# Weight and activation tiles moved by 64 bytes, and the squares of the norm in another ring: a two-layer decoder trunk on one core

## The chip, the cores and the metric

The kernel runs on 1 core of one Trainium2 chip. The metric is device time in microseconds, from the runs' median. Five engines work side by side, each in the order of its own queue: TensorE (PE, its weight loads shown apart as PEld), VectorE (DVE), ScalarE (ACT), GpSimd (POOL) and SyncE (SP), which issues most transfers.

## What is computed

A trunk of two layers on 512 tokens of width 1024, all in float32. Cut to what matters here:

```python
def hybrid_layer(x, norm_mix, w_in, ..., w_out, norm_mlp, w_up, w_down):
    h = rmsnorm(x, norm_mix)
    proj = h @ w_in                 # 1024 x 4896: queries, keys, values, gates
    ...                             # forgetting attention -> y_a, sparse attention -> y_b
    mixed = jax.nn.sigmoid(gate_a) * y_a + jax.nn.sigmoid(gate_b) * y_b
    x = x + mixed @ w_out
    h = rmsnorm(x, norm_mlp)
    return x + jnp.square(jax.nn.relu(h @ w_up)) @ w_down    # 1024 -> 4096 -> 1024

def reference(x, ...):
    for l in range(2):
        x = hybrid_layer(x, ...)
    return rmsnorm(x, norm_final)

def rmsnorm(x, g):
    return x * lax.rsqrt(jnp.mean(x * x, axis=-1, keepdims=True) + 1e-6) * g
```

## The kernel before

**Layout of the work.** Activations stand transposed: features on the 128 partitions, the 512 tokens along the free axis, so that x is eight tiles of 128 x 512. Every matrix product is made of three products of reduced-precision parts: a value v is split into a high part h (a cast) and a low part v - h, and weight-high by activation-high, weight-high by activation-low and weight-low by activation-high are added in PSUM. In `gemm` these are lines 244, 245 and 246. The activation is the moving operand (128 x 512), the weight block the stationary one (128 x 128).

**Tiles.** `Body.t(tag, shape)` gives out tiles by tag. Each tag has a number of buffers in `BUFS`; tags in `LOCAL` get the part of the program appended, so that "t2" is one ring in the attention of layer 0 ("a0") and another in its output projection and MLP ("m0"). Where a tile lies in SBUF is worked out by the framework's packer at build time: a tag's count limits how many of its tiles are alive, and any tile may be put into bytes whose owner is no longer alive, whatever its tag; it then has to wait for the last use of those bytes. All sizes are multiples of 2048 bytes a partition save one: the tile "tiny" (small vectors and constants) is 6976 bytes, which is 54.5 times 128. In the program before the packer puts the large rings below it, at multiples of 128 bytes (the double tiles "u2", the rings "kd", "kk", "long" and "vn", a part of the "o2" tiles), and the others above it, where every address is 64 past a multiple of 128 (the weight tiles "wh" and "wl", most of "o2", the late activations "a4", the raw weights "e", "f" and "raw").

**The tags that the change touches.**
- "u2" (4 buffers, 8192 bytes): holds u, the normed input's high and low parts, two feature tiles to a buffer, made by `make_u` through `twin` (lines 266 to 279). u is the moving operand of the projections of a layer (`block`, lines 244 to 246) and the stationary one in `token_proj` (lines 368 to 370). In the MLP the same ring holds split weights: in `Strassen.convert` (line 1497) the pairs a11 and a12, s1 and a22, s2 and s4 for the up-projection, in `Strassen.operands` (line 1252, through `twin`) the operands d for the last quarter of the down-projection. The operand s3 goes into a single tile of the ring "zz".
- "a4" (4 buffers, 6144 bytes): the late activations (the last four of the sixteen units), made in `Strassen.act` and moved in `Strassen.down` as a11, a12 and s4; s1, s2, s3 and a22 move the combined tiles "tt".
- "tmp" (3 buffers): short-lived 128 x 512 tiles, among them the squares and their running sum in `sumsq`.
- "t2" (12 buffers a part): the scratch of `Strassen.prepare` in the MLP parts.

**Order of the work around the change.** After the attention, a loop over m from 0 to 7 does the output projection, one feature tile at a time: 24 matmuls, the residual sum on VectorE (line 1094), then `S.prepare(m)`, which makes the Strassen operands of x (line 1424 scales, lines 1416 and 1417 split into high and low), then `sumsq`, which squares x[m] on ScalarE (line 288) and adds the square to the running sum (line 298), on GpSimd unless its argument `last` is set. From m = 4 on a step of the first unit's weight conversion is put between. The MLP's up-projection is done as sixteen Strassen units (`unit`): seven products (`narrow`, line 1523) of 12 matmuls of 128 x 256, with the down-projections of earlier units put between them (`DOWNS`). The last quarter of the down-projection is Strassen's form too (`down`, line 1315). Its end in layer 0 (`whole`) squares and sums x once more, makes u for layer 1 and sends x to memory.

The order of an engine's instructions is the framework's: it starts from the order of the source and lets its planner move ready work ahead.

Of the kernel before, what the change touches and what calls it, by code (L numbers as in the profile page):

```python
# [19 lines left out]
T = 512  # L20
# [117 lines left out]
def run(*gens):  # L138
    for g in gens:
        for _ in g:  # L140
            pass


class Body:
# [13 lines left out]
    def t(self, tag, shape, dt=F32, name=None):  # L158
        if tag in self.TINY:
            n, bufs = self.TINY[tag]  # L160
            o = self.offset[tag] + self.turns[tag] % bufs * n
            self.turns[tag] += 1
            v = self.tiny[:, o:o + int(np.prod(shape[1:]))]
            return v.rearrange("p (a b c) -> p a b c", a=shape[1], b=shape[2]) if len(shape) == 4 else \
                v.rearrange("p (a b) -> p a b", a=shape[1]) if len(shape) == 3 else v
        n = int(np.prod(shape[1:]))
        if tag in ("tmp", "small") and n < T:
            v = self.sb.tile([128, T], dt, name=name or tag, tag=tag, bufs=self.BUFS[tag])[:, :n]
            if len(shape) > 2:
                v = v.rearrange("p (a b) -> p a b", a=shape[1])  # L170
            if len(shape) > 3:
                raise ValueError(shape)
            return v
        bufs = self.BUFS[tag]
        if tag in self.LOCAL:
            bufs = self.BUFS.get(tag + self.part[0], bufs)
            tag += self.part
        return self.sb.tile(shape, dt, name=name or tag, tag=tag, bufs=bufs)


    LOCAL = "f", "kd", "kk", "q2", "vn", "hl", "zz", "pt", "t2", "zc", "tt"
# [99 lines left out]
    def sumsq(self, x, acc, last=False, behind=None):  # L281

        nc = self.nc
        n = x.shape[-1]
        s = self.t("zz" if last == "apart" else "tmp", [128, T], name="sq")[:, :n]
        if behind is not None:
            nc.scalar.copy(s[:, :1], behind[:, :1].bitcast(F32))
        nc.scalar.activation(s, x, AF.Square)
        if not acc:
            self.sums = 0  # L290
            return [s]
        self.sums += 1
        if self.sums == 6 and len(acc) == 1:
            self.table(AF.Sqrt, s)
        if last == "apart":
            return acc + [s]
        o = self.t("tmp", [128, T], name="acc")[:, :n]
        (nc.vector if last else nc.gpsimd).tensor_tensor(o, s, acc[0], op=OP.add)
        return [o] + acc[1:]
# [321 lines left out]
    def compress(self, kc, vc, small, l):  # L621
# [3 lines left out]
        for x, pos in ((kc, "pos_k"), (vc, "pos_v")):  # L625
            t = [self.t("t2", [128, 8, 2, 32], name="ca") for _ in range(2)]
            v = x.rearrange("p (n j r) -> p r j n", j=8, r=2)
            for half in range(2):
                nc.vector.memset(t[half][:, :, 1, 31], 0.0)
                o = OFF[pos] + 8 * half  # L630
                nc.vector.tensor_copy(t[half][:, :, 0, 31], small[:, o:o + 8])
                for h in range(2):
                    for r in range(2):
                        copy = nc.scalar.copy if h else nc.vector.tensor_copy
                        copy(t[half][r * 64:(r + 1) * 64, :, h, :31], v[h * 64:(h + 1) * 64, r, :, half:half + 31])
            A.append(t)
            yield
# [224 lines left out]
    def layer(self, l, u):  # L862
        nc, a = self.nc, self.a
        self.part = f"a{l}"
        wb = a["wb"][l].rearrange("m p k c -> m p (k c)")

        va = [self.p(t) for t in ("S", "S", "PT", "PT")]
        src = [[a["wva"][l, c].rearrange("p j m -> p (j m)")] for c in range(4)]
        if l == 0:
# [6 lines left out]
        run(g)  # L876
        small = self.small
        g2 = [self.p(t) for t in ("mm", "mm", "O", "O")]
        g = self.token_proj([[a["wg2"][l, c].rearrange("p j m -> p (j m)")] for c in range(4)], 288, g2, u)
        VF = []  # L880
        for b in range(NB):
            v = self.t("va", [128, 8, 128], F32R, name="vf")
# [7 lines left out]
        z = self.t("z", [128, NB, 8])  # L890
# [188 lines left out]
        x = [self.t("pt", [128, 2, T], name="x") for _ in range(KT // 2)]  # L1079
        x = [t[:, i] for t in x for i in range(2)]  # L1080
# [8 lines left out]
        acc = []  # L1089
        for m in range(8):  # L1090
            ps = self.bank()
            w = self.weights(a["wout"][l, m].rearrange("p k c -> p (k c)"))
            run(self.gemm(ps, w, 0, mixed))
            nc.vector.tensor_add(x[m], x[m], ps)
            S.prepare(m)
            acc = self.sumsq(x[m], acc, m == 7)
            if m > 3:
                next(conv, None)
        run(conv)
# [539 lines left out]
```

## Time and profile before

| | us |
|---|---|
| median of 3 runs (1528.76 to 1532.7) | 1531.52 |
| the profiled execution, whole | 1529.82 |
| its span, first to last instruction | 1528.0 |
| TensorE busy | 1505.8 |
| VectorE busy | 1153.5 |
| ScalarE busy | 807.9 |
| GpSimd busy | 139.7 |

The span is taken on the device between the first and the last instruction of the program; the 1.8 us more of the execution lie around it. In rows of groups the columns are: source line, engine, operation, output tile <- input tiles (buffer numbers left out), shape of output <- input, count | busy time in us, mean duration in ns | idle time of the engine just before, and what ended it. In rows of the timeline: start in us from the span's start, length in us, engine, line, operation, tiles, shape, count, and in brackets the idle time before with its releaser. Matmuls are pipelined: the duration of one is longer than the step from its start to the next one's start. In rows of waits: who waited for whom: total in us, times, longest.

### The profile page before, as it was taken

The numbers are of one execution on the slowest core, as the hardware profiler recorded it, in microseconds if no ns is written. First come the engines' busy times: TensorE is split into PE (matmuls) and PEld (weight loads), VectorE is DVE, ScalarE is ACT, GpSimd is POOL, SyncE is SP. The second block draws the span as 40 slices with busy tenths as digits, with TensorE's granted clock in tenths as the row PEclk, the third lists the DMA queues.
The fourth block names the chain that finished last, engine by engine and source line by source line (L and its number), as shares of the span: only waits on it lengthen the run. The fifth ranks groups of instructions, "written<-read, shape, count | busy, mean of one in ns | idle before, by whom it ended". The sixth has DMA issues, their size and how long they took to land.

```text
span 1528.0 us, 23442 instructions
## 1 busy us (share of the span) xinstructions
PE 1505.8 (99%) x8766; PEld 1308.7 (86%) x8766; DVE 1153.5 (75%) x2237; ACT 807.9 (53%) x1536; POOL 139.7 (9%) x169
## 2 busy tenths in 40 slices
PE   9999999999989999999999999999999999999998
PEld 8877888888888989999988788888887899999998
DVE  5678979777876776678747789787779677677796
ACT  6465655554664444455444556565547554444455
POOL 1010000000310000010220000000014100000111
PEclk9999999999999999999999999999999999999999
DMA  7664422224655554564167553222346554544532
GB/s 269 163 165 125 138 69 71 68 73 153 189 145 144 146 138 132 143 167 118 55 207 190 151 123 106 83 70 69 104 156 167 131 158 132 147 145 133 137 98 69
DMA packets 73922, 200.51 MB, mean 131 GB/s; under 512 B 9264, under 2 KB 10672, under 8 KB 73808
## 3 DMA queue, kind: packets, MB, share of 16 engines
q1 hardware_dynamic: 58256, 171.19, 35.9%
q0 software_dynamic: 11520, 20.98, 8.0%
q10 hardware_dynamic: 4032, 6.84, 1.3%
q8 instruction: 69, 1.13, 0.3%
q14 instruction: 45, 0.37, 0.1%
HBM read 150.67 MB, written 4.19 MB: 101 GB/s over the span
## 4 chain that ended last, share of the span: by engine, by line
PE 93%; DVE 3%; issue 1%; ACT 1%; DMA 1%; POOL 1%; POOLq 0%; SPq 0%; DVEq 0%; ACTq 0%
PE ps_mm L244 11%; PE ps_mm L245 11%; PE ps_mm L246 11%; PE ps_S L1523 9%; PE ps_PT L1523 6%; PE ps_mm L1523 4%; PE ps_O L244 4%; PE ps_O L245 4%; PE ps_O L246 4%; PE ps_O L612 2%; PE ps_PT L586 2%; PE ps_S L561 2%; PE ps_O L1523 2%; PE ps_S L1315 2%; PE ps_mm L1315 2%
## 5 line engine op out<-in xcount | busy, mean ns | idle before, releaser
L218 ACT CAST wh<-raw 128x1024 fp32r<-128x1024 f32 (+2 forms) x161 | 164.5, 1024 | 145.4 <-PE ps_mm L245 44.6
L219 DVE TENSOR_TENSOR wl<-raw,wh 128x1024 fp32r<-128x1024 f32 (+2 forms) x161 | 191.7, 1191 | 26.0 <-ACT wh L218 25.3
L1504 DVE TENSOR_TENSOR s<-raw,s 128x1024 fp32r<-128x1024 f32 (+1 forms) x128 | 138.7, 1087 | 89.4 <-ACT s L1503 89.1
L244 PE MATMUL ps_mm<-u,wh 128*128 128x512 f32 x480 | 193.9, 404 | 0.0
L246 PE MATMUL ps_mm<-u,wl 128*128 128x512 f32 x480 | 190.8, 397 | 0.0
L245 PE MATMUL ps_mm<-u,wh 128*128 128x512 f32 x480 | 190.8, 397 | 0.0
L1503 ACT CAST s<-raw 128x1024 fp32r<-128x1024 f32 (+1 forms) x128 | 119.1, 940 | 28.4 <-PE ps_mm L1523 17.0
L244 PE MATMUL ps_mm<-o,wh 128*128 128x512 f32 x288 | 113.5, 394 | 0.0
L245 PE MATMUL ps_mm<-o,wh 128*128 128x512 f32 x288 | 113.2, 393 | 0.0
L246 PE MATMUL ps_mm<-o,wl 128*128 128x512 f32 x288 | 113.1, 393 | 0.0
L244 PE MATMUL ps_O<-o,wh 128*128 128x512 f32 x280 | 110.3, 394 | 0.1
L245 PE MATMUL ps_O<-o,wh 128*128 128x512 f32 x280 | 110.2, 393 | 0.0
L246 PE MATMUL ps_O<-o,wl 128*128 128x512 f32 x280 | 110.0, 393 | 0.0
L1523 PEld LDWEIGHTS ps_S<-t,s 128*128 128x128 f32 x768 | 101.2, 193 | 8.4 <-ACT z L1553 3.7
L246 PEld LDWEIGHTS ps_mm<-u,wl 128*128 128x128 f32 x480 | 90.2, 188 | 20.3
L1523 PE MATMUL ps_S<-t,s 128*128 128x256 f32 x768 | 104.7, 285 | 2.8 <-ACT z L1553 2.8
L244 PEld LDWEIGHTS ps_mm<-u,wh 128*128 128x128 f32 x480 | 90.5, 188 | 18.9 <-issue 0.8
L245 PEld LDWEIGHTS ps_mm<-u,wh 128*128 128x128 f32 x480 | 90.4, 188 | 17.0 <-issue 0.4
L1599 ACT ACTIVATE z<-z 128x512 f32<-128x512 f32 x64 | 40.5, 633 | 93.0 <-DVE z L1598 92.8
L590 ACT CAST pth<-ps_PT 128x384 fp32r<-128x384 f32 (+1 forms) x96 | 48.9, 512 | 66.1 <-PE ps_PT L586 66.1
L548 DVE CUSTOM_DVE_ANT_0 E<-ps_S,ct 128x384 f32<-128x384 f32 (+3 forms) x112 | 57.3, 514 | 32.6 <-PE ps_S L561 31.3
L549 ACT ACTIVATE E<-E,tiny 128x384 f32<-128x384 f32 (+3 forms) x112 | 65.6, 585 | 20.4 <-DVE tiny L548 20.1
(356 smaller groups left out, 3434.2 us busy)
## 6 DMA issues: line engine op xcount, KB each, us to landing
raw<-wb SPq DMA_DIRECT2D x64, 512.0 KB, 3.3
raw<-wup SPq DMA_DIRECT2D x64, 512.0 KB, 4.4
raw<-wd SPq DMA_DIRECT2D x48, 512.0 KB, 3.6
raw<-raw POOLq DMA_DIRECT2D x80, 256.0 KB, 3.4
w<-w SPq DMA_DIRECT2D x32, 256.0 KB, 5.1
kda<-hla SPq DMA_DIRECT2D x32, 256.0 KB, 4.2
q2a<-hla SPq DMA_DIRECT2D x64, 128.0 KB, 2.3
raw<-wo SPq DMA_DIRECT2D x16, 512.0 KB, 4.3
```

The source lines that it names most:

```text
L218: nc.scalar.copy(h[:, :n], raw[:, :n])
L219: nc.vector.tensor_tensor(lo[:, :n], raw[:, :n], h[:, :n].bitcast(F32), op=OP.subtract)
L244: mm(ps, h[:, c], xh, start=start and i == 0, stop=False)
L245: mm(ps, h[:, c], xl, start=False, stop=False)
L246: mm(ps, lo[:, c], xh, start=False, stop=stop and i == ks - 1)
L548: nc.vector.tensor_tensor_reduce(e, ps, self.mask[:, T - n:], -1.0, BIG, OP.add, OP.min, mx)
L549: nc.scalar.activation(e, e, AF.Exp, bias=mx, scale=-1.0, accum_out=un["sm"][:, i:i + 1])
L590: nc.scalar.copy(h[:, e, :n], ps[:, :n])
L1315: mm = lambda o, *z, **kw: nc.tensor.matmul(o, *z, skip_group_check=True, **kw)
L1503: nc.scalar.copy(h, src)
L1504: nc.vector.tensor_tensor(lo, src, h.bitcast(F32), op=OP.subtract)
L1523: mm = lambda o, *z, **kw: self.nc.tensor.matmul(o, *z, skip_group_check=True, **kw)
```

## The change

- Tiles with the tags "u2" and "a4" are asked for with 32 elements more (128 bytes), and the kernel uses their middle, from element 16 on: they lie 64 bytes past the place that the packer gives them. With the packer's places as described, u and the double weight tiles then lie 64 bytes past a multiple of 128, and the late activations at a multiple.
- In the output projection and the MLP of both layers the squares of `sumsq` come from the ring "t2" of that part instead of "tmp". The running sum stays in "tmp".
- In the loop of the output projection the seventh feature tile's sum (m = 6) is VectorE's too, beside the eighth's; before it was GpSimd's.

```diff
@@ -175,7 +175,13 @@
         if tag in self.LOCAL:
             bufs = self.BUFS.get(tag + self.part[0], bufs)
             tag += self.part
+        if tag[:3] in self.SHIFT:
+            v = self.sb.tile([128, n + 32], dt, name=name or tag, tag=tag, bufs=bufs)[:, 16:16 + n]
+            dims = dict(zip("abc", shape[1:-1]))
+            return v.rearrange(f"p ({' '.join(dims)} z) -> p {' '.join(dims)} z", **dims) if dims else v
         return self.sb.tile(shape, dt, name=name or tag, tag=tag, bufs=bufs)
+
+    SHIFT = "u2", "a4"
@@ -282,7 +288,7 @@
-        s = self.t("zz" if last == "apart" else "tmp", [128, T], name="sq")[:, :n]
+        s = self.t("zz" if last == "apart" else "t2" if self.part[0] == "m" else "tmp", [128, T], name="sq")[:, :n]
@@ -1093,7 +1099,7 @@
             run(self.gemm(ps, w, 0, mixed))
             nc.vector.tensor_add(x[m], x[m], ps)
             S.prepare(m)
-            acc = self.sumsq(x[m], acc, m == 7)
+            acc = self.sumsq(x[m], acc, m > 5)
             if m > 3:
                 next(conv, None)
```

## The prediction

> **What bounds the kernel now.** I read span and clock first, then busy time per engine and the chain that ended last on the page.
>
> ```profile
> core 0: 1528.0 us, clock 0.996
> ```
> ```profile
> PE 1505.8 (99%) x8766; PEld 1308.7 (86%) x8766; DVE 1153.5 (75%) x2237; ACT 807.9 (53%) x1536; POOL 139.7 (9%) x169
> ...
> PE 93%; DVE 3%; issue 1%; ACT 1%; DMA 1%; POOL 1%; POOLq 0%; SPq 0%; DVEq 0%; ACTq 0%
> ```
>
> TensorE is busy for 99% of the span, at a granted clock of 0.996, and carries 93% of the chain. So only two things can move the time: how long a matmul takes when nothing is late, and the few places where TensorE stands still. The change touches both.
>
> For the first I read the groups of TensorE with shapes kept apart: same line, same weight tiles, same 128x512 form, and only the moving operand differs.
>
> ```profile
> L245 PE MATMUL ps_mm<-u,wh 128*128 128x512 f32 x480 | 190.8, 397 | 0.0
> L245 PE MATMUL ps_mm<-o,wh 128*128 128x512 f32 x288 | 113.2, 393 | 0.0
> ```
>
> A matmul that moves u lasts 397 ns, one that moves o 393. Durations overlap, so what counts is the step from start to start. I take it from the timeline of TensorE, over runs that nothing interrupts. The layout of the program (not in the profile) puts u, the double weight tiles, the Strassen operands in the "kd" and "long" rings and a few o tiles at multiples of 128 bytes, and wh, wl, most o tiles and the late activations 64 past.
>
> ```profile
> 42.78 0.39 PE L244 MATMUL ps_PT<-u,wh 128*128 128x512 f32 x1
> ...
> 53.98 0.39 PE L244 MATMUL ps_mm<-u,wh 128*128 128x512 f32 x1
> ```
>
> Here 48 matmuls move u, from a multiple of 128: 11.20 us, 233.3 ns each. The next four rows are two runs of 12 on one source line, in one stage, both moving an o tile; the first lies 64 past, the second at a multiple.
>
> ```profile
> 478.31 0.39 PE L244 MATMUL ps_O<-o,wh 128*128 128x512 f32 x1
> ...
> 481.05 0.40 PE L1523 MATMUL ps_PT<-b,s 128*128 128x256 f32 x2
> ```
> ```profile
> 715.68 0.40 PE L244 MATMUL ps_O<-o,wh 128*128 128x512 f32 x1
> ...
> 718.48 0.75 PE L1315 MATMUL ps_PT<-ohl,d 128*128 128x256 f32 x5
> ```
>
> 2.74 us / 12 = 228.3 ns against 2.80 / 12 = 233.3, the same as u. So the place of the moving tile goes with 5 ns of 233, whatever the tile holds. For 256 columns the down stage of layer 0 shows it in one stretch, 12 matmuls a row:
>
> ```profile
> 727.00 1.58 PE L1315 MATMUL ps_PT<-tt,d 128*128 128x256 f32 x12
> 728.42 1.58 PE L1315 MATMUL ps_O<-tt,d 128*128 128x256 f32 x12
> 729.83 1.60 PE L1315 MATMUL ps_PT<-tt,d 128*128 128x256 f32 x12
> 731.27 1.60 PE L1315 MATMUL ps_O<-tt,d 128*128 128x256 f32 x12
> 732.71 1.60 PE L1315 MATMUL ps_PT<-tt,d 128*128 128x256 f32 x12
> 734.15 1.60 PE L1315 MATMUL ps_O<-tt,d 128*128 128x256 f32 x12
> 735.59 1.58 PE L1315 MATMUL ps_PT<-ohl,d 128*128 128x256 f32 x12
> 737.01 1.57 PE L1315 MATMUL ps_O<-ohl,d 128*128 128x256 f32 x12
> ```
>
> The first two are s3, whose weights are a single tile lying 64 past: steps 1.42 and 1.41 us. The next four are a22 and s1, weights in double tiles at a multiple and moving tiles at a multiple too: 1.44 each. The last pair moves the late activations (64 past) over double weights: 1.42. So at 256 columns it is both at a multiple that costs, 1.44 - 1.415 = 0.025 us per 12, or 2.1 ns.
>
> Then the places where TensorE stands still, from its waits:
>
> ```profile
> PE ps_mm L1523 <- ACT b L1416: 7.4, 2, 4.0
> PE ps_S L1523 <- ACT z L1553: 2.8, 2, 1.4
> PE ps_S L1315 <- DVE x L1334: 1.8, 1, 1.8
> PE ps_O L1315 <- ACT d L1253: 1.4, 1, 1.4
> ```
>
> The largest, twice, is the step from the output projection into the MLP; the last two are the end of layer 0.
>
> **The change part by part.**
>
> *u 64 bytes on.* u is the moving operand of 1440 matmuls into mm (480 on each of lines 244 to 246) and of 96 into PT (48 a layer, the run from 42.78 and its twin): 1536. Bounds for one: 4 ns (397 against 393, a mean in which some o tiles lie at a multiple) and 5 ns (the two runs of 12). I take 4.3, nearer the mean over many: 1536 x 4.3 = 6.6 us off, bounds 6.1 and 7.7. As stationary operand in the token projections (384 matmuls at lines 368 to 370) u goes from a multiple to 64 past while wh moves at 64 past. That pair is the one o already has with wh (228.3), so I take 0, with bounds of 2.1 ns either way, 0.8 us.
>
> *Double weight tiles 64 bytes on, up-projection.* Line 1523 runs 2 x 16 units x 7 products x 12 = 2688; s3 uses a single tile, so 2304 are concerned. For a22, s1 and s2 (1152) the moving tile is at a multiple: 1152 x 2.1 = 2.4 us off. For a11, a12 and s4 the half of a11 and a12 in the "vn" ring is also at a multiple: 384 x 2.1 = 0.8 off. The other 768 move from 64 past, and get weights at 64 past: no row of 256 columns has that pair. Its nearest row is the 512-column run at 228.3, which has both at 64 past and is the fast one: 0, bounds 2.1 ns either way, so 1.6 us.
>
> *The same, down-projection.* 672 at line 1315; 288 of them move "tt" over double tiles: 0.6 us off. The 288 that move the late activations exchange places, 64 past over a multiple for a multiple over 64 past: 1.42 against 1.415 in the rows above, so 0. Sum of the phases: 6.6 + 2.4 + 0.8 + 0.6 = 10.4 us.
>
> Writing the shifted tiles on ScalarE and VectorE costs nothing: the split of a weight tile at a multiple and 64 past takes the same.
>
> ```profile
> L219 DVE TENSOR_TENSOR wl<-raw,wh 128x1024 fp32r<-128x1024 f32 x151 | 184.3, 1220 | 19.4 <-ACT wh L218 18.8
> L1504 DVE TENSOR_TENSOR s<-raw,s 128x1024 fp32r<-128x1024 f32 x96 | 117.1, 1221 | 89.4 <-ACT s L1503 89.1
> ```
>
> *The seventh sum of squares to VectorE.* In layer 0 GpSimd works on it for 4.61 us, and a ScalarE cast of the last operands waits for it, though it needs none of its data (by the layout, the old sum that it reads lies in the bytes that the cast writes):
>
> ```profile
> 415.53 4.61 POOL L298 TENSOR_TENSOR acc<-sq,acc 128x512 f32<-128x512 f32 x1 [5.04 <-ACT sq L288]
> ```
> ```profile
> 420.17 0.62 ACT L1416 CAST t<-ts 128x512 fp32r<-128x512 f32 x1 [2.29 <-POOL acc L298]
> ```
> ```profile
> 420.82 0.69 DVE L1417 TENSOR_TENSOR t<-ts,t 128x512 fp32r<-128x512 f32 x1 [1.82 <-ACT t L1416]
> ```
>
> VectorE idles 1.82 us for that cast, with the residual sum of the last block (line 1094) behind it, which the operands of the waiting product need. Without GpSimd these 1.82 go. The sum itself then costs VectorE one instruction:
>
> ```profile
> 1182.93 0.68 DVE L298 TENSOR_TENSOR acc<-sq,acc 128x512 f32<-128x512 f32 x1
> ```
>
> If it stands ahead of that residual sum, 0.68 is late again; the scheduler may put it behind. I take the cautious case: 1.82 - 0.68 = 1.1 off in layer 0. In layer 1 the same sum held up nobody: VectorE runs into the residual sum without a gap (the row has no idle time behind it), so there 0.68 is added.
>
> ```profile
> 1178.10 0.67 DVE L1094 TENSOR_TENSOR x<-x,ps_S 128x512 f32<-128x512 f32 x1
> ```
>
> Behind the sum on VectorE stand the residual sum and line 1417's splits, and TensorE for them; behind the old one on GpSimd stood only a transfer that waited for VectorE anyway. Together 0.4 off; bounds 1.4 slower (both sums in the way) and 7.4 faster (both waits gone).
>
> *Squares in the "t2" ring.* They leave "tmp" (3 buffers: old sum, square, new sum) for a ring of 12, whose load in that stage is at most 8 kept tiles, 2 new ones and 2 squares. That is full but not over, so I cost waits for it at nothing; the cover is the 24 matmuls of one block (24 x 0.228 = 5.5 us). What goes is ScalarE's wait for a buffer at the end of layer 0:
>
> ```profile
> 738.67 0.64 ACT L288 ACTIVATE sq<-x 128x512 f32<-128x512 f32 x1 [0.45 <-POOL acc L298]
> ...
> 740.99 0.63 ACT L288 ACTIVATE sq<-x 128x512 f32<-128x512 f32 x1 [0.56 <-POOL acc L298]
> ...
> 742.14 0.60 ACT L1253 CAST d<-raw 128x512 fp32r<-128x512 f32 x1
> ```
>
> 0.45 + 0.56 = 1.0 us earlier for the cast at 742.14, which TensorE waits 1.4 for. I take 1.0 off, bounds 0 and 3.2 (1.4 + 1.8); late next is VectorE's split of u, which competes there with GpSimd.
>
> **Sum:** 10.4 + 0.4 + 1.0 = 11.8 us off. The profiled execution took 1529.8 us (span 1528.0 and 1.8 around it), 1.7 below the median of 1531.5. It becomes 1518.0, and the median 1519.7.
>
> [...]
>
> **The rivals.**
>
> *A: the phases pay, the rest does not.* The 768 with both at 64 past lose 2.1 ns (1.6 us), both sums stand in VectorE's way (1.4), and the end of layer 0 stays: 1531.5 - 10.4 + 1.6 + 1.4 = 1524.1. For it: no row has that pair at 256 columns. Chance 0.17.
>
> *B: the waits go as well.* All 7.4 + 3.2 us fall away: 1531.5 - 10.4 - 10.6 = 1510.5; half of them 1515.8. For it: two of the waits start from GpSimd sums and shared buffers. Against: VectorE is busy without a gap ahead of the one in layer 1. Chance 0.14.
>
> *C: the place is not the cause*, u being slow for something else that its stage has: only the waits' 1.4, so 1530.1, no measurable change. [...] Against: the o tiles at a multiple step at 233.3 in another stage, like u. Chance 0.06.
>
> *D: slower.* The longer tiles take 8 x 128 bytes of a memory that is packed full, and sharing of bytes makes a ScalarE step late in every Strassen unit, as it does now once in a layer at line 1553 (1.4 us). From 9 further units of the 30 the gain of 11.8 is gone; in half of them, 15 x 1.4 = 21 us come back: 1540.7. Against: these waits are at 2 of 32 units now, and 1 KB is small beside a 4 KB tile. Chance 0.06.
>
> **How the numbers follow.** My forecast has 0.57, A 0.17, B 0.14, C 0.06, D 0.06. About 0.3% (4.6 us) can be told from no change. Faster, under 1526.9: forecast, A, B, less a part of A's upper end, 0.85. Same: C and that part, 0.09. Slower: D, 0.06. The range leaves out C, D and the lower half of B: 1512 to 1527.
>
> **What would show it.** Steps of u runs at 228 instead of 233 ns, and 393 instead of 397 in the groups; rows of 12 with "tt" at 1.42 instead of 1.44; no GpSimd sum at the seventh block and a wait for line 1416 under 7.4 us; no ScalarE wait for GpSimd's sums. Wrong it would be if u's groups stay at 397, or if new waits of TensorE appear inside the Strassen units.

## The result, and the profile after

The changed kernel takes 1517.46 us in the median (four runs, 1516.49 to 1518.59), the kernel before, run beside it, 1531.47. The ratio is 0.9911, 95% interval 0.9894 to 0.9928: faster by 0.9%, 2.2 us below the forecast and inside its range. The profiled execution took 1518.59 us, its span is 1516.8, against 1528.0 before. From line 181 on the line numbers of the changed kernel are 6 higher than before (line 245 is 251, 1416 is 1422, 1523 is 1529).

The page after, span and clock, busy times and the chain:

```profile
core 0: 1516.8 us, clock 0.995
```
```profile
PE 1500.2 (99%) x8766; PEld 1301.5 (86%) x8766; DVE 1153.2 (76%) x2239; ACT 809.0 (53%) x1536; POOL 128.7 (8%) x167
...
PE 93%; DVE 3%; ACT 2%; issue 1%; DMA 0%; POOL 0%; SPq 0%; POOLq 0%; ACTq 0%; DVEq 0%
```

TensorE is still the bound and its busy time fell by 5.6 of the 11.2 us. The rest is standing still. GpSimd lost 11 us, which counts for nothing by itself.

The groups of TensorE with shapes kept apart, first two rows of before that were not shown yet, then four of after:

```profile
L245 PE MATMUL ps_O<-o,wh 128*128 128x512 f32 x280 | 110.2, 393 | 0.0
...
L1523 PE MATMUL ps_S<-t,s 128*128 128x256 f32 x768 | 104.7, 285 | 2.8 <-ACT z L1553 2.8
```
```profile
L251 PE MATMUL ps_mm<-u,wh 128*128 128x512 f32 x480 | 190.0, 396 | 0.0
...
L251 PE MATMUL ps_mm<-o,wh 128*128 128x512 f32 x288 | 113.1, 393 | 0.0
...
L251 PE MATMUL ps_O<-o,wh 128*128 128x512 f32 x280 | 110.8, 396 | 0.0
...
L1529 PE MATMUL ps_S<-t,s 128*128 128x256 f32 x768 | 101.5, 280 | 0.4 <-ACT z L1559 0.4
```

This is not what was forecast. u fell by 1 ns and not by 4. The output projection's o, whose tag was not touched, rose from 393 to 396. The up-projection fell by 5 ns, more than twice the 2.1 in the sum.

TensorE's waits after:

```profile
PE ps_O L252 <- DVE wl L225: 1.8, 1, 1.8
PE ps_S L252 <- DVE wl L225: 1.8, 1, 1.8
PE ps_S L1321 <- DVE x L1340: 1.8, 1, 1.8
...
PE ps_PT L1321 <- DVE d L1260: 0.8, 1, 0.8
PE ps_O L1321 <- ACT d L1259: 0.7, 1, 0.7
```

The largest wait of before, 7.4 us at the step into the MLP, is gone altogether. In its place TensorE waits twice for a weight split on VectorE (line 225), once a layer, inside the output projection.

**Where the 11 us went.** I took every step of TensorE from start to start in both traces. What of a step lies over 243 ns at 512 columns, or over 137 at 256, I count as standing still or as a low clock; the rest is the step itself.

| us | forecast | measured |
|---|---|---|
| steps of u's matmuls | -6.6 | -2.7 |
| steps of o's matmuls | 0 | +1.7 |
| steps of the up-projection | -3.2 | -5.1 |
| steps of the down-projection's quarter | -0.6 | -1.2 |
| standing still and low clock, up-projection (16.0 to 2.9) | -0.4 | -13.0 |
| the same, output projection and o's other matmuls (2.0 to 7.7) | 0 | +5.7 |
| the same, end of layer 0 and of layer 1 (5.4 to 6.0) | -1.0 | +0.6 |
| everything else | 0 | +3.2 |
| sum | -11.8 | -10.9 |

Of the last +3.2, 1.4 are waits in the token projections. Another 0.9 lies at the program's end: in this execution the clock fell before the last eight matmuls (line 339), which take 2.07 us, for 1.16 before (line 333). The rest is spread over small matmuls and was not followed up.

**The low clock.** The mean of 0.995 hides that the low clock comes in pieces. Stretches of the changed kernel (us from:to, length, busy time and count of TensorE, its weight loads, VectorE, ScalarE and GpSimd, then granted clock, DMA share, GB/s) around the first wait for line 225, which begins at 410.7:

```profile
412.00:413.50 1.50, 0.97 (x4) 0.84 (x5) 1.50 (x3) 0.00 (x0) 0.00 (x0) 1.00 0.00 0
413.50:417.25 3.75, 3.75 (x11) 2.89 (x11) 3.75 (x9) 3.50 (x6) 0.00 (x0) 0.54 0.74 217
417.25:420.00 2.75, 2.75 (x17) 2.35 (x16) 2.75 (x5) 1.63 (x4) 0.00 (x0) 1.00 0.53 176
```

And of before, behind its 4.0 us wait for line 1416:

```profile
424.20:427.60 3.40, 3.40 (x18) 3.40 (x17) 3.40 (x8) 2.04 (x5) 0.00 (x0) 0.51 0.99 231
```

In half-microsecond windows the clock there is 0.50 and beside it 1.00. The lost time of one such piece is 1.71 us wherever I added it up: 3.4 us at half speed. So a wait of TensorE with such a piece behind it costs 1.7 us more than its row says. Before had one piece behind each of the two waits for line 1416, so the step into the MLP cost 7.4 + 3.4 = 10.8 us. After has 3.7 + 1.7 = 5.4 in the output projection. Most of the difference of the waits is these 5.4 us; the wait for z (line 1553, now 1559), 2.8 before and 0.4 after, is the next.

In the changed kernel the low clock followed a wait of 1.84 us (410.68 to 412.52) and began at about 413.8, 1.2 us behind the wait's end. In before the wait of 4.05 us ended at 423.74 and the low clock began at about 424.1.

### The profile page after: what moved, and what is told of

It is laid out like the page before. It is cut to its first block, busy times and chain, and to the rows that moved or that the text cites. A ratio compares the mean times of both kernels' runs of the same rounds, so it can differ in the third digit from the quotient of the medians.

```text
span 1516.8 us, 23457 instructions
## 1 busy us (share of the span) xinstructions
PE 1500.2 (99%) x8766; PEld 1301.5 (86%) x8766; DVE 1153.2 (76%) x2239; ACT 809.0 (53%) x1536; POOL 128.7 (8%) x167
## 4 chain that ended last, share of the span: by engine, by line
PE 93%; DVE 3%; ACT 2%; issue 1%; DMA 0%; POOL 0%; SPq 0%; POOLq 0%; ACTq 0%; DVEq 0%
PE ps_mm L250 12%; PE ps_mm L251 11%; PE ps_mm L252 11%; PE ps_S L1529 9%; PE ps_PT L1529 6%; PE ps_O L250 4%; PE ps_O L252 4%; PE ps_O L251 4%; PE ps_mm L1529 4%; PE ps_O L618 2%; PE ps_PT L592 2%; PE ps_S L567 2%; PE ps_S L1321 2%; PE ps_mm L1321 2%; PE ps_O L1529 1%; PE ps_O L492 1%
## 5 line engine op out<-in xcount | busy, mean ns | idle before, releaser
L1529 PE MATMUL ps_S<-t,s 128*128 128x256 f32 x768 | 101.5, 280 | 0.4 <-ACT z L1559 0.4
```

The costliest lines, as they stand in the source:

```text
L1529: mm = lambda o, *z, **kw: self.nc.tensor.matmul(o, *z, skip_group_check=True, **kw)
```

## The experiments

Three theories stood at the start.

- **P**: a matmul's step depends on the distance from the moving tile's place to the place of the next weights, modulo 256 bytes. It came from the traces of before and after: the added 128 bytes make the pitch of the ring 8320 bytes, 32.5 times 256, so that its tiles lie alternately at 64 and at 192 modulo 256.
- **M**: only the place modulo 128 counts, as in the prediction.
- **S**: the waits carry the gain.

**The places alone.** The sums and the ring as before.

```diff
-        s = self.t("zz" if last == "apart" else "t2" if self.part[0] == "m" else "tmp", [128, T], name="sq")[:, :n]
+        s = self.t("zz" if last == "apart" else "tmp", [128, T], name="sq")[:, :n]
-            acc = self.sumsq(x[m], acc, m > 5)
+            acc = self.sumsq(x[m], acc, m == 7)
```

> The two tiles moved by 64 bytes, squares and seventh sum as before. Theory P (a matmul's step depends on the distance between the places of its moving tile and of the next weights, counted modulo 256 bytes): steps as in the changed kernel, 8.3 us less than before when each distance is given the step that both traces show for it; the waits of the step into the MLP stay at 10 us, so 1531.5 - 8.3 = 1523.2. Rival M (only modulo 128: at 512 columns the moving tile's place, at 256 columns both at a multiple): also 1521 to 1523, as in the prediction's sum of the phases. Rival S (the waits carry the gain): 1529 or more.

1521.38 us against 1531.92 of before, ratio 0.9936 (0.9921 to 0.9952). S falls. The waits into the MLP stayed:

```profile
PE ps_mm L1529 <- ACT b L1422: 8.0, 2, 4.5
```

P (1523.2) and M (1521 to 1523) both allow this time, so the run does not tell them apart. The profiled execution took 1526.5, the longest of six: it has two pieces of low clock, back to back, behind each of these waits and again at the end of layer 0. That is three pieces, 5.1 us, more than before.

**The sums and the ring alone.**

```diff
-    SHIFT = "u2", "a4"
+    SHIFT = ()
```

> Squares in the other ring and the seventh sum on VectorE, no tile moved. Theory P and rival M: steps as before (u at 233), waits from 10.4 us to about 4, less what a lower clock after a new wait costs: 1526 to 1528. Rival S: 1520 or less.

1525.32, ratio 0.9961 (0.9949 to 0.9974), and S falls again. The median is 0.7 us under what P and M gave for it. Both halves of the change pay by themselves, 10.5 and 6.6 us in the medians; their sum of 17.1 is more than the 14.0 of both together. The waits for line 225 are here too (1.9 and 2.7), so they come with the sums or the ring and not with the places.

**All double tiles at the weights' place modulo 256.**

```diff
-            v = self.sb.tile([128, n + 32], dt, name=name or tag, tag=tag, bufs=bufs)[:, 16:16 + n]
+            v = self.sb.tile([128, n + 64], dt, name=name or tag, tag=tag, bufs=bufs)[:, 16:16 + n]
```

> The changed kernel with the moved tiles 256 bytes longer in place of 128, so that all tiles of a ring lie at the same place modulo 256 (u and the weight tiles wh, wl then all at 192), still 64 past a multiple of 128. Theory P: u's matmuls step at 227 to 228 ns in place of 231, the half of the up-projection that had weights at 64 gets them at 192, in sum 7.8 us less than the changed kernel: 1509.7. Rival M: nothing changes modulo 128, 1517.5.

**All double tiles at multiples of 256.**

```diff
-            v = self.sb.tile([128, n + 32], dt, name=name or tag, tag=tag, bufs=bufs)[:, 16:16 + n]
+            v = self.sb.tile([128, n + 64], dt, name=name or tag, tag=tag, bufs=bufs)[:, 32:32 + n]
```

> As the one before with the tiles moved by 128 bytes in place of 64: u and the double weight tiles lie at multiples of 128 as before the change, but at 0 modulo 256 in place of 128. Theory P: u steps at 229 ns, the up-projection's matmuls at 118.6 in place of 119.8; in sum within 1 us of the changed kernel, 1516.5. Rival M: all is at multiples of 128 again, u at 233 and the up-projection at 119.8, so only the waits' gain stays: 1526 to 1528.

They took 1515.27 (ratio 0.9895, 0.9882 to 0.9908) and 1519.67 (0.9926, 0.9913 to 0.9939). The totals lie between the theories; the steps decide. The same run of 48 matmuls that move u, first and 49th row of TensorE's timeline, in the changed kernel, at the weights' place, and at multiples of 256:

```profile
44.11 0.40 PE L250 MATMUL ps_PT<-u,wh 128*128 128x512 f32 x1
...
55.18 0.39 PE L250 MATMUL ps_mm<-u,wh 128*128 128x512 f32 x1
```
```profile
43.18 0.39 PE L250 MATMUL ps_PT<-u,wh 128*128 128x512 f32 x1
...
54.09 0.39 PE L250 MATMUL ps_mm<-u,wh 128*128 128x512 f32 x1
```
```profile
43.32 0.40 PE L250 MATMUL ps_PT<-u,wh 128*128 128x512 f32 x1
...
54.32 0.39 PE L250 MATMUL ps_mm<-u,wh 128*128 128x512 f32 x1
```

11.07, 10.91 and 11.00 us, or 230.6, 227.3 and 229.2 ns a step, where before had 233.3. In the third run u lies at a multiple of 128, just as before, and is 4 ns faster than before. M has no room for that and falls. That the place of the weights counts as well, and not the moving tile's alone, shows in the token projections. There wh moves, from 192 modulo 256 in the kernel before and in these two runs, and only the place of u, the weights, differs. The 32 matmuls `ps_PT<-wh,u` of line 376 (370 before) last 389 ns on average with u at 192, 391 with u at 128 and 395 with u at 0. The places are the packer's and stand in no profile. Sorted by distance, in stretches where neither place changes:

| distance (moving - next weights), mod 256 | 512 columns, ns | 256 columns, ns |
|---|---|---|
| 0 | 228 to 229 | 119.4 to 119.8 |
| 64 | 229 to 230 | 116.6 to 118.8 |
| 128 | 232 | 118 to 119 |
| 192 | 233 to 233.5 | 115.5 to 116.7 (118.3 once) |

These are means from the four traces, of 64 to 2360 steps each at 512 columns and of 18 to 1801 at 256 (a distance of 0 between tiles at place 64, 14 steps, left out). At 512 columns equal places are the best case, at 256 columns the worst. Why the sign turns is not known, nor what makes the distance matter at all; the runs show only that it does.

The run at the weights' place did not reach P's 1509.7, although its steps were right, and the run at multiples of 256 ended 3.2 us over P's 1516.5. Their waits had grown. In the first:

```profile
PE ps_O L252 <- DVE wl L225: 2.9, 1, 2.9
PE ps_S L1529 <- ACT z L1559: 2.8, 2, 1.4
PE ps_S L252 <- DVE wl L225: 2.6, 1, 2.6
```

Each of the two waits for line 225 has a piece of low clock behind it. Its steps are together 7.6 us shorter than the changed kernel's, and TensorE waits longer for the same VectorE. The second run waits 3.0 and 2.3 us for line 225 and 2.8 for line 1559.

**Sum and ring apart.** Two kernels with the change less one edit. Both get another packing from the program's layout, in which every o tile has the weights' place. By the distances that is worth 3.7 us to both.

```diff
 seventh sum back on GpSimd:
-            acc = self.sumsq(x[m], acc, m > 5)
+            acc = self.sumsq(x[m], acc, m == 7)
 squares back in "tmp":
-        s = self.t("zz" if last == "apart" else "t2" if self.part[0] == "m" else "tmp", [128, T], name="sq")[:, :n]
+        s = self.t("zz" if last == "apart" else "tmp", [128, T], name="sq")[:, :n]
```

> The changed kernel with the seventh sum back on GpSimd; the squares keep their own ring. The packer gives this program other places for o: all of them lie at the place of the weights, so that the sum of the matmuls' steps by their distances modulo 256 bytes is 3.7 us below the changed kernel's. Theory K (the ring alone keeps ScalarE from queueing the operand b behind GpSimd's sum): the wait for line 1422 stays under 1 us and the time is 1517.5 - 3.7 = 1514, 1511.5 to 1516.5 by what the wait for line 225 in the output projection does. Rival G (it is GpSimd's own lateness, and the sum on VectorE was what removed the wait): the wait for line 1422 is back with 7 to 8 us and the time is 1519 to 1523.

> The changed kernel with the squares back in the ring of the running sums; the seventh sum stays on VectorE. Same places as the run with the sum on GpSimd (o at the weights' place, 3.7 us of steps less than in the changed kernel). Theory K (the ring is what removed the wait for line 1422): the wait is back in part, 3 to 8 us, and the time is 1517 to 1522. Rival G (the sum on VectorE removed it): the wait stays under 1 us, the time is 1511.5 to 1516.5. Both edits sufficient each by itself: both runs under 1516.5.

With the ring alone 1516.11 (ratio 0.9920, 0.9905 to 0.9934), with the sum alone 1514.89 (0.9910, 0.9895 to 0.9925); this chip gave before 1528.54, 3 us less than the other. Their waits, ring alone first:

```profile
PE ps_S L252 <- DVE wl L225: 2.9, 1, 2.9
PE ps_O L252 <- DVE wl L225: 2.5, 1, 2.5
```
```profile
PE ps_mm L1529 <- ACT b L1422: 4.0, 2, 2.0
```

The waits support K: the sum alone takes the wait for line 1422 from 8.0 (both edits undone) to 4.0, and with the ring it is gone. How much of that is the ring's own is less sure, since TensorE then arrives there later by the waits for line 225. The times do not decide. As they stand, both lie under 1516.5, which was the sign for either edit being enough by itself; by their ratios, on the scale of the first chip, they are 1519.2 with the ring alone, above K's range, and 1517.7 with the sum alone, in K's. And it is the ring that brings the wait for line 225. VectorE's timeline shows how. The changed kernel, then the one without the ring:

```profile
405.91 0.68 DVE L1100 TENSOR_TENSOR x<-x,ps_S 128x512 f32<-128x512 f32 x1
406.51 1.72 DVE L1510 TENSOR_TENSOR s<-raw,s 128x1024 fp32r<-128x1024 f32 x1
...
409.83 1.50 DVE L1426 SCALAR_TENSOR_TENSOR b<-bs,b 128x256 fp32r<-128x256 f32 x1
411.26 1.21 DVE L225 TENSOR_TENSOR wl<-raw,wh 128x1024 fp32r<-128x1024 f32 x1
```
```profile
405.24 0.67 DVE L1100 TENSOR_TENSOR x<-x,ps_S 128x512 f32<-128x512 f32 x1
405.84 1.21 DVE L225 TENSOR_TENSOR wl<-raw,wh 128x1024 fp32r<-128x1024 f32 x1
...
407.72 1.54 DVE L1443 TENSOR_TENSOR ts<-bs,ts 128x256 f32<-128x256 f32 x1
```

Without the ring the weight split stands right behind the residual sum, as before. With it a split of Strassen weights and six operand steps stand ahead of it, and TensorE needs it first. Its input was there: the cast of wh on ScalarE ended at 406.51.

```profile
405.47 1.04 ACT L224 CAST wh<-raw 128x1024 fp32r<-128x1024 f32 x1
```

The two programs differ by the ring's edit and by the packing that follows. The kernel with the ring alone has the packing of the second for o and the order of the first:

```profile
404.42 0.67 DVE L1100 TENSOR_TENSOR x<-x,ps_S 128x512 f32<-128x512 f32 x1
405.02 2.07 DVE L1510 TENSOR_TENSOR s<-raw,s 128x1024 fp32r<-128x1024 f32 x1
...
410.10 1.21 DVE L225 TENSOR_TENSOR wl<-raw,wh 128x1024 fp32r<-128x1024 f32 x1
```

So the order is the planner's answer to the ring. ScalarE's order moves as well, to the good: before, the square stands ahead of the cast of b that TensorE waits for; after, behind it.

```profile
422.78 0.61 ACT L288 ACTIVATE sq<-x 128x512 f32<-128x512 f32 x1
423.30 0.39 ACT L1416 CAST b<-bs 128x256 fp32r<-128x256 f32 x1
```
```profile
422.51 0.41 ACT L1422 CAST b<-bs 128x256 fp32r<-128x256 f32 x1
...
424.06 0.63 ACT L294 ACTIVATE sq<-x 128x512 f32<-128x512 f32 x1
```

Here too the ring decides: with the ring alone the square starts 1.55 us behind that cast (422.04 against 420.49), with the sum alone 0.52 us ahead of it (418.82 against 419.34).

**All seven sums on VectorE**, with the change's 128 bytes and with 256:

```diff
-            acc = self.sumsq(x[m], acc, m > 5)
+            acc = self.sumsq(x[m], acc, True)
```

> The changed kernel with all seven sums of the output projection's loop on VectorE, same places of all operands. Theory V (the new wait for line 225 inside the output projection is VectorE's two-input operation of line 1426 taking 1.50 us beside a sum on GpSimd instead of 0.41, and the low clock right behind that wait follows from it): line 1426 takes 0.41 to 0.45 in that place, the waits for line 225 (1.8 + 1.8) go or fall under 1 us together, no window at a granted clock under 0.9 follows, and the time is 1517.5 - 3.6 - 1.6 = 1512.3, 1511 to 1514. Rival Q (VectorE's queue is simply too long there: the sum takes 0.68 us of it in place of the 1.09 us lost): waits for line 225 of 2 to 4 us remain, the time is 1516 to 1519.

> The kernel with 64 elements of padding (the double tiles all at the weights' place modulo 256 bytes, the late activations too), and all seven sums of the output projection's loop on VectorE. Theory V: the waits for line 225 (2.9 + 2.6 there) fall under 1 us together and the two stretches at a low clock go: 1515.3 - 5 - 3 = 1507, 1505.5 to 1510. Rival Q: waits for line 225 of 3 us and more remain, 1513 to 1517. In both the matmuls that move u step at 227 to 228 ns.

1513.98 (ratio 0.9904, 0.9888 to 0.9921) and 1508.18 (0.9868, 0.9854 to 0.9883). In both the wait for line 225 is gone, line 1426 takes 0.42 us, and no low clock follows anywhere between the output projection and the first units. Q's waits did not come. The times say less: as they stand they lie in V's ranges, but this chip is the faster one, and by their ratios they are 1516.8 and 1511.3 on the scale of the first chip, the one in Q's range and the other between the two. V's rows came out, its reason only in part: in the kernel without the ring VectorE also loses 1.1 us beside a sum on GpSimd (the row at 407.72), and nobody waits. Taking the sums off GpSimd changed the planner's order once more, and the split stands right behind the residual sum again. So the order makes the wait, and the row of 1.50 us beside a sum, for 0.42, makes it longer by up to 1.1 us; that is an estimate from these two rows, for a kernel with the bad order and no such row was not run. The wait for line 1422 is absent here too, with the ring and without a wait for line 225 ahead of it. A part of the gain comes back as ScalarE's, 1.4 us in each layer with 128 bytes:

```profile
PE ps_S L1529 <- ACT z L1559: 2.7, 2, 1.4
```

Since the chips differ by 3 us, the changed kernel and these two were run once more side by side.

> The changed kernel itself, beside the next two on one chip, since the chip of the runs with all sums on VectorE gave the kernel before 1528.5 and not 1531.5. Both theories: 0.991 of before; the waits for line 225 1.8 and 1.8 again, one or two stretches at a low clock behind them.

> All seven sums on VectorE, 64 bytes as in the changed kernel. By the waits and the low clock that its profile had lost (3.6 + 1.6) less what came back as the wait for line 1559 (2.7 for 0.4): 1.6 to 3 us under the changed kernel on the same chip. Theory Q': the wait only moves, the same within 1 us.

> 64 elements of padding and all seven sums on VectorE, beside the changed kernel on one chip. Sum of the matmuls' steps by their distances 7.8 us under the changed kernel's, waits and low clock 2 to 3 us under it: 7.5 to 11 us below the changed kernel. If only distances modulo 128 bytes mattered, up-projection and u would be as in the changed kernel and only 2 to 3 us would be left.

1517.76, 1514.83 and 1509.10 us (ratios 0.9923, 0.9906 and 0.9864 to before's 1530.04, interval of the last 0.9845 to 0.9882). All sums on VectorE are worth 2.9 us, and the weights' place with them 8.7, both as expected for this comparison; V's sum before it had put the first at 5.2. The last is the fastest version of this study: 1.4% under before, where the change has 0.8% on the same chip.

## Why the prediction was right, and where it was not

**The bound and the sign** held: TensorE is busy for 99%, and steps and waits are all that moved. The place of a tile is worth several microseconds here: the run with the places alone took 1521.4, for 1531.9 of before beside it, where rival C would have been 1530.1.

**u 64 bytes on** is the step that failed. The prediction divided places by 128. Its two kinds of rows (228.3 and 233.3) were really the distances 0 and 192 modulo 256, and it missed that u's 64 bytes more come with a pitch that isn't a multiple of 256. Half of u's tiles went to distance 0, the other half to 128, and 233.3 became 230.6 in the run of 48, not 228. So 2.7 us came for 6.6. With the pitch at 8448 bytes the step comes out, 227.3 ns in that run of 48, and u's matmuls gain 5.3 us in all, still under the lower bound of 6.1. The prediction's own sign of being wrong, u's groups staying at 397, came close: they went to 396.

**o** was not in the sum. In the changed program's packing a part of the o tiles lies at distance 128 or 192 from the weights, more than before, +1.7 us. In the two programs of "sum and ring apart", which have the same longer tiles, all o tiles are at distance 0: the packing is not steered by the edit alone.

**Double weight tiles**: -5.1 for -3.2. The size of 2.1 ns came from two rows of 12; over 805 and 595 steps the pairs with t (distance 192 and 64) are 116.0 and 116.8 ns where before, at distance 0, had 119.7. And the 768 with both at 64 past were costed at nothing as the fast pair: at 256 columns the equal pair is a slow one (119.4). This term and u's missed in opposite directions. The slow equal pair is what rival A named.

**The seventh sum** removed what it should: no GpSimd sum there, no 1.82 us gap in VectorE. The cautious case happened, the sum stands in the queue ahead of the residual sum:

```profile
416.74 0.68 DVE L304 TENSOR_TENSOR acc<-sq,acc 128x512 f32<-128x512 f32 x1
...
419.68 0.68 DVE L1100 TENSOR_TENSOR x<-x,ps_O 128x512 f32<-128x512 f32 x1
```

But 0.4 us was far too little: the wait for line 1422 is 8.0 us with neither edit and 4.0 with the sum alone (in another packing), and the low clock behind a wait was not in any term.

**The "t2" ring** was costed only at the end of layer 0. There ScalarE's wait for GpSimd went as forecast, and nothing came of it: ScalarE now waits 1.34 us for VectorE, whose step ahead of that x takes 1.78 us beside a sum on GpSimd (0.68 for the same step before, line 1254). The next sum runs beside a split of u, which the prediction named as next and which takes 2.24 us there (in before 2.23 beside a sum, at 742.42, and 0.74 without one, at 741.43), and behind that split stands the x that TensorE waits 1.8 us for. Rows of GpSimd, VectorE and ScalarE together:

```profile
733.53 1.40 POOL L304 TENSOR_TENSOR acc<-sq,acc 128x512 f32<-128x512 f32 x1 [0.30 <-ACT sq L294]
733.70 1.78 DVE L1260 TENSOR_TENSOR d<-raw,d 128x512 fp32r<-128x512 f32 x1
735.40 0.41 DVE L1359 TENSOR_TENSOR x<-x,ps_O 128x256 f32<-128x256 f32 x1
735.85 0.63 ACT L294 ACTIVATE sq<-x 128x512 f32<-128x512 f32 x1 [1.34 <-DVE x L1359]
...
737.33 2.24 DVE L284 SCALAR_TENSOR_TENSOR u<-x,tiny,u 128x512 fp32r<-128x512 f32 x1
739.50 0.41 DVE L1340 TENSOR_TENSOR x<-x,ps_PT 128x256 f32<-128x256 f32 x1
```

Its real effect was on the order of two queues in the output projection, about 4 us of waits less at line 1422 and 3.7 more at line 225, and no part of the prediction looked there. "Waits for it at nothing" was right for the buffers and wrong for the plan.

So the forecast of 1519.7 holds, but that it came within 2.2 us is in good part luck, since its terms offset one another: steps 3.1 us worse than forecast, waits with their clock 5.3 better, 3.2 lost elsewhere, which makes 10.9 of 11.8 in the profiled pair. The medians differ by 14.0, since the profiled execution of before lies 1.7 under its median and that of after 1.1 over. Rival B's half (1515.8) describes the waits best, together with u at less than half its price. Rival D did not happen: the wait for line 1553 went from 2.8 to 0.4.

Not settled: why z at line 1559 waits 0.4 in some of these kernels and about 2.8 in others, in part in kernels with equal waits ahead of it; and why the sign of the place effect turns between 256 and 512 columns.

## What to carry to other kernels

Where TensorE is busy all the time, tabulate its start-to-start steps by the places of the moving tile and of the next weights at the finest grain that the layout has (here 64 bytes in 256, not in 128), for each column count by itself, and work out the pitch of a ring, not only its first tile. An edit that only renames a buffer's ring can reorder other engines' queues; look for the first instruction that TensorE needs in each queue, not for the buffer. Price a wait of TensorE with the low clock that may follow it: here 1.7 us a piece, with all ten waits of 2.5 us and more at lines 225 and 1422 and with three of the eight of 1.8 to 2.3.

## What the hardware showed that was not expected

- Steps of 128 x 512 matmuls go from 227 to 233.5 ns with the distance of two tiles modulo 256 bytes, and of 128 x 256 matmuls from 115.5 to 119.8 in nearly the opposite order.
- The granted clock falls to 0.50 for 3.4 us, or twice that, close behind some waits of TensorE: in before and the changed kernel it fell 0.3 to 1.4 us after the end of the wait for line 225 or line 1416, with the ring alone as much as 0.8 us ahead of it (from about 1161.9, in a wait that lasted to 1162.7). In nine traces there are eighteen waits of 1.8 us and more at line 225 or line 1422 (1416 of before). Thirteen had such a piece about or behind their end: all ten of 2.5 us and more, three of the eight shorter ones. Three were followed by two pieces (waits of 3.5, 4.5 and 2.9 us). No piece was seen there in the four traces without such a wait. The length of one wait is not the whole condition. At the end of layer 0 (line 1315 of before, 1321 after) two waits stand close together, of 0.7 to 1.4 and of 1.8 to 2.4 us, and all thirteen traces have a low clock there, three of them for 6.8 us. What exactly sets it off is not settled.
- Operations of VectorE on 128 x 256 with two inputs (lines 1426 and 1443) took 1.48 to 1.54 us in seven rows of four traces (1.43 to 2.32 in six rows of before, lines 1420 and 1437), and 0.41 to 0.42 elsewhere: all of these long rows stand beside such a sum. Not every one beside a sum is long: in before four such operations (lines 1417, 1420 and 1437, 415.85 to 417.27) took 0.41 us each while the sum on GpSimd beside them took 4.61 us (from 415.53), for 1.29 of the sum ahead of it (409.19). What decides which of the two is slow was not shown.
